# Where the time steps of a state-space layer stand: a new order at the seam of two layers in a one-core Trainium2 kernel

## The chip, the core and the metric

The kernel runs on one core of a Trainium2 chip. The metric is the device time of one execution in microseconds, as the median of several runs. Five engines work from queues of their own, each in its order: TensorE (PE in the profile, its weight loads PEld), VectorE (DVE), ScalarE (ACT), GpSimd (POOL), and SyncE (SP), which here issues most transfers. An instruction that waits holds up all that stands behind it on its engine.

## The reference

Two layers on a latent stream of 1024 tokens by 1024 features and a context of 256 tokens. Layer 0 is gated windowed attention with rotary positions. Layer 1, of which the change moves the beginning, is a gated bidirectional state-space mixer with 8 groups of 4 heads, head size 64, state size 128, chunks of 128 tokens. Cut to what matters:

```python
z, xbc, dt_raw = jnp.split(h @ w_in, [SSD_WIDTH, SSD_WIDTH + SSD_CONV_DIM], axis=-1)
xbc = jax.nn.silu(centred_depthwise_conv(xbc, conv_w, conv_b))      # 5 taps
xs, bm, cm = jnp.split(xbc, [...])
dt = jax.nn.softplus(dt_raw + dt_bias_dir)                          # time steps, 64 = 2 directions x 32 heads
...
da = dt * a_dir ; a_cs = cumsum(da) in chunks of 128                # per direction
states = einsum(bm, exp(a_last - a_cs), xs * dt)
# scans over the chunks: first the 2 of the context, then the 8 of the latents
y = y_diag + y_off ; u = (y + d_skip * xs) * silu(z) ; grouped norm ; @ w_out
```

The time steps `dt` are needed by every group; `xs`, `bm`, `cm` and `z` belong to a group.

## The kernel before

Features lie on the partitions, tokens along the free axis, in three pieces `TT`: tokens 0 to 511 (i = 0), 512 to 1023 (i = 1) and the context (i = 2). Every product is done three times in a reduced float format, high by high, high by low and low by high, so operands are split into `uH`, `uL` and `wh`, `wl`: ScalarE casts the high part, VectorE or GpSimd subtracts the low one.

The end of layer 0 is `out_steps(1)` in `attention` (L836 to L838): for each of eight output tiles it loads two weight halves (`wr`, L219, split at L212 and L214), multiplies (L226 to L228), adds the gated result to the residual `h1k` on VectorE (L760), squares it on ScalarE (L767) and adds the square to `sqa` on GpSimd (L768). Then `fin` sums the squares over partitions with a product by ones (L258), takes the root on ScalarE (L260), the reciprocal on VectorE (L261) and modulates the eight tiles of piece 1 into `uH`, `uL` (L293 to L295).

`ssd_consts` comes next. It loads the time steps' weights (`wdth`, `wdtl`), multiplies them with pieces 2, 0 and 1 into `psX` (L899, recorded as L226 to L228), evicts to `dt` (L900) and runs softplus, logarithm, scans and exponentials on the 64 rows, in tiles `w` (L906 to L952). There are two such chains, an early one over pieces 0 and 2 (768 columns) and a late one over piece 1 (512 columns). Split rows go out to DRAM (`rowh`, `rowl`, L927 to L932). At the end each chunk's values are transposed so that tokens lie on partitions: TensorE (L956, L959, L960) into `psX`, ScalarE from there into `dtdec`, `eacs` and `dtb` (L957, L961, L962). `psX` has three buffers, and a transpose into a tile waits for an earlier copy out of the same tile.

`front(g)` makes a group's inputs: tile 0 (`bT`), tiles 1 and 2 (the two halves of `xs`, through `cacc`), tile 3 (`cT`) and then z. Tiles 0 to 2 also have a context product into `psD` (24 matmuls of 256 columns, L1046); then 48 matmuls of 512 columns for the latents into `pj2` (L1055). Their finish is queued as steps in `post`: five taps (one on ScalarE L968, four on VectorE L972), silu (tanh on ScalarE L979, the product on VectorE L980), and `natural`, the transposes that put tokens on partitions (TensorE L1019, copies on ScalarE L1022). `post.run(cost)` emits steps as the front's matmuls go on, by an estimated cost of each matmul. `states(0)` follows as soon as tile 2 is done: per chunk a weighting on GpSimd (L1130), a product (L1153) and a decay and add.

The order on each engine isn't the order of this code: the program is built with `schedule_with_timeline_sim=True`, where a scheduler orders all instructions by its own estimates. `issue_after` and priorities restrict it.

Of the kernel before, what the change touches and what calls it, by code (L numbers as in the profile page):

```python
# [9 lines left out]
F32 = mybir.dt.float32  # L10
BF16 = mybir.dt.bfloat16
F32R = mybir.dt.float32r
# [5 lines left out]
P = 128  # L18
# [41 lines left out]
LATE = 3.0  # L60
SEGS = (1.5, 2.0, 2.0, 2.2, 2.2)
# [42 lines left out]
class Kernel:  # L104
# [117 lines left out]
    def mm3(self, ps, pairs, first=True, last=True):  # L222

        n = len(pairs)
        for i, (lh, ll, rh, rl) in enumerate(pairs):
            self.nc.tensor.matmul(ps, lh, rh, start=first and i == 0, stop=False)  # L226
            self.nc.tensor.matmul(ps, lh, rl, start=False, stop=False)  # L227
            self.nc.tensor.matmul(ps, ll, rh, start=False, stop=last and i == n - 1)  # L228
# [493 lines left out]
    def attention(self, c0, ckv):  # L722
# [21 lines left out]
        def out_steps(i):  # L744
# [4 lines left out]
            def one(m):  # L749
# [15 lines left out]
                else:  # L765
                    sq = t(p, [P, n], F32, "ut")
                    nc.scalar.activation(sq, h1, AF.Square)  # L767
                    nc.gpsimd.tensor_tensor(st["acc"], st["acc"], sq, op=ALU.add)  # L768
# [80 lines left out]
    def ssd_consts(self, p):  # L849
# [3 lines left out]
        dr = self.dr  # L853
# [17 lines left out]
        self.acs_d = t(dr, [2, 64, LAT], F32, "acs")  # L871
        self.v_d = t(dr, [2, 64, LAT], F32, "vrow")
# [3 lines left out]
        eal_d = t(dr, [1, 64, NT], F32, "eald")  # L876
        q = self.pdt
        wr = t(self.wp, [P, KT, P], F32, "wr")[:, :, :64]
# [15 lines left out]
        keep = keep.rearrange("p c n -> p (c n)")  # L894
        dts = t(q, [64, LAT + CTX], F32, "dt")
        where = {0: 0, 2: 512, 1: 768}
        for i in (2, 0, 1):
            n = TT[i][1]
            pj = self.proj(ps, (wh, wl), i, tag="psX", m=64)  # L899
            nc.scalar.activation(dts[:, where[i] : where[i] + n], pj[:64, :n], AF.Identity, bias=db)  # L900
        for lo, n, chunks in ((0, 768, (0, 1, 2, 3, 8, 9)), (768, 512, (4, 5, 6, 7))):
            nb = n // P
            dt = dts[:, lo : lo + n]
            if lo:
                q = self.pool("dtp2", ctx=self.cdt, side="right")
            w1, w2, w3 = [t(q, [64, n], F32, x) for x in ("w1", "w2", "w3")]  # L906

            nc.vector.scalar_tensor_tensor(w1, in0=dt, scalar=-1.0, in1=dt, op0=ALU.mult, op1=ALU.min)
            nc.scalar.activation(w1, w1, AF.Exp)
            nc.vector.tensor_scalar_add(w2, w1, 1.0)  # L910
            nc.vector.tensor_scalar_add(w3, w2, -1.0)
            nc.vector.tensor_sub(w1, w1, w3)
            nc.scalar.activation(w2, w2, AF.Ln)
            nc.scalar.activation(w3, w2, AF.Exp, scale=-1.0)
            nc.vector.tensor_mul(w1, w1, w3)
            nc.vector.tensor_add(w1, w1, w2)
            nc.vector.scalar_tensor_tensor(dt, in0=dt, scalar=0.0, in1=w1, op0=ALU.max, op1=ALU.add)
            ln = w2
            nc.vector.tensor_scalar_max(ln, dt, 1.0e-38)
            nc.scalar.activation(ln, ln, AF.Ln)  # L920
            da = w1
            nc.vector.tensor_scalar(out=da, in0=dt, scalar1=al, scalar2=None, op0=ALU.mult)
            acs = w3
            nc.vector.tensor_tensor_scan(out=acs[:32], data0=keep[:32, :n], data1=da[:32], initial=0.0, op0=ALU.mult, op1=ALU.add)
            nc.vector.tensor_tensor_scan(out=acs[32:, ::-1], data0=keep[32:, :n][:, ::-1], data1=da[32:, ::-1], initial=0.0, op0=ALU.mult, op1=ALU.add)
            def rows(dst, src):
                h = t(q, [64, 512], F32R, "rowh", 2)  # L927
                l = t(q, [64, 512], F32R, "rowl", 2)
                nc.scalar.copy(h, src[:, :512])
                nc.vector.tensor_sub(l, src[:, :512], h)  # L930
                for x, y in enumerate((h, l)):
                    nc.sync.dma_start(dst[x, :, chunks[0] * P : chunks[0] * P + 512], y.bitcast(F32))  # L932

            rows(self.acs_d, acs)
            av = acs.rearrange("p (c n) -> p c n", n=P)
            tot = t(q, [64, 6], F32, "tot")[:, :nb]
            nc.vector.tensor_copy(tot[:32], av[:32, :, P - 1])
            nc.vector.tensor_copy(tot[32:], av[32:, :, 0])
            et = t(q, [64, 6], F32, "et")[:, :nb]
            nc.scalar.activation(et, tot, AF.Exp)  # L940
            nc.sync.dma_start(eal_d[0][:, chunks[0] : chunks[0] + 4], et[:, :4])
            if nb > 4:
                nc.sync.dma_start(eal_d[0][:, 8:10], et[:, 4:])

            nc.vector.tensor_sub(ln, ln, acs)
            rows(self.v_d, ln)

            dd = w1
            nc.vector.tensor_sub(dd.rearrange("p (c n) -> p c n", n=P), tot.unsqueeze(2).broadcast_to([64, nb, P]), av)
            nc.scalar.activation(dd, dd, AF.Exp)  # L950
            nc.vector.tensor_mul(dd, dd, dt)
            nc.scalar.activation(acs, acs, AF.Exp)  # L952
# [10 lines left out]
        nc.sync.dma_start(self.eal, eal_d.broadcast_to([P, 64, NT]))  # L963
# [18 lines left out]
    def front(self, g, st, post, first=None):  # L982
# [21 lines left out]
        def need(w):  # L1004
            while "l" not in w:
                post.pop()
# [30 lines left out]
        for n, (x, kind) in enumerate(tiles):  # L1037
            need(w)
            cur, w = w, loads[n + 1]()
            nat = {"bT": ("bn", 0), 0: ("xn", 0), 1: ("xn", P)}.get(kind)  # L1040
            wh, wl = cur["h"], cur["l"]
            if nat:
                raw = t(ps, [P, 512], F32, "psD")[:, :CTX]
                for k in range(KT):
                    for y, (l, r) in enumerate(((wh, uH), (wh, uL), (wl, uH))):
                        nc.tensor.matmul(raw, l[:, k, :], r[2][:, k, :], start=k + y == 0, stop=k == KT - 1 and y == 2)  # L1046
                        yield N256
                acc = t(pf, [P, CTX], F32, "cctx")
                post.extend(self.taps(x, raw, acc, 0, CTX, CTX) + self.silu(raw, acc) + natural(raw, acc, [(st[nat[0]][2], 0, 2)], nat[1], 2))
            raw = t(ps, [P, LAT], F32, "pj2")  # L1050
            acc = t(pf, [P, LAT], F32, "cacc") if nat and kind != "bT" else t(p, [P, LAT], F32, kind)
            for k in range(KT):
                for y, (l, r) in enumerate(((wh, uH), (wh, uL), (wl, uH))):
                    for i in range(2):
                        nc.tensor.matmul(raw[:, 512 * i : 512 * i + 512], l[:, k, :], r[i][:, k, :], start=k + y == 0, stop=k == KT - 1 and y == 2)  # L1055
                        yield N512
                if k == 3:
                    post.extend(w["steps"])
# [563 lines left out]
```

## Time and profile before

| what | value |
|---|---|
| median of 3 runs (lowest to highest) | 1857.68 us (1857.05 to 1858.12) |
| the profiled execution, its own time | 1859.69 us |
| its span, first to last instruction | 1858.0 us |
| mean granted TensorE clock | 0.988 |
| TensorE busy | 1778.6 us (96%) |
| VectorE, ScalarE, GpSimd busy | 1176.4, 902.9, 731.7 us |
| layer 0's last sum of squares (L258) | at 752.7 us |
| first time-step transpose (L956) | at 793.4 us |
| tile 2 of the first front starts | at 813.9 us |
| first z product (L1080) | at 843.8 us |

How to read the rows below: a row of an engine has the start and the length in microseconds, the engine, the line of the kernel, the operation, what it writes and reads, the shape, and in brackets how long the engine was idle before it and what ended that. The row of tenths cuts the span in 40 slices, a digit being the busy tenths of a slice (9 is 90% or more); the row PEclk is the clock that TensorE was granted, in tenths. A matmul's length includes its way through the array, so matmuls in a row overlap, and what one costs is the distance between their starts. A wait is put down to what came last by the profile.

### The profile page before, as it was taken

The page shows a single profiled execution, that of the slowest core. Times are in us where ns is not written, and L with a number is a line of the kernel's source. Part 1 is how long each engine was busy: PE and PEld are TensorE (multiplying, and loading weights), DVE is VectorE, ACT ScalarE, POOL GpSimd, SP SyncE. Part 2 cuts the span into 40 slices and gives each one's busy share as a digit, 9 for nine tenths or more (in the row PEclk, how much of TensorE's full clock was granted, in tenths as well). Part 3 has the DMA queues.
Part 4 walks back from the last instruction along what each step waited for, and adds up shares of the span by engine and source line. Part 5 has one row for each costly group of instructions (what it writes and reads, how often), then busy time and mean ns, then how long its engine had stood idle before and what let it go on. Part 6 is the DMA issues. An engine that isn't in the chain of part 4 may idle for free. (4 is left out here: it accounts for less than half of the span.)

```text
span 1858.0 us, 29740 instructions
## 1 busy us (share of the span) xinstructions
PE 1778.6 (96%) x10684; PEld 1537.0 (83%) x10684; DVE 1176.4 (63%) x2208; ACT 902.9 (49%) x1858; POOL 731.7 (39%) x1007
## 2 busy tenths in 40 slices
PE   6999999999999998979999999999999999999997
PEld 4797877788898786768898898989889898988886
DVE  3654438777778666773766657576665757754743
ACT  3522336677788664552444435344443534543532
POOL 2441137654466454103252443525344352542411
PEclk9999999999999999989999999999999999999998
DMA  7767866443355447021111111111111111433552
GB/s 294 278 170 251 272 167 151 106 116 97 90 136 121 127 129 229 17 65 35 30 40 52 33 47 33 48 33 39 53 34 47 34 47 34 155 109 98 176 161 72
DMA packets 145492, 196.30 MB, mean 106 GB/s; under 512 B 15393, under 2 KB 84897, under 8 KB 144321
## 3 DMA queue, kind: packets, MB, share of 16 engines
q1 hardware_dynamic: 111280, 175.76, 30.2%
q0 software_dynamic: 34064, 18.65, 5.5%
q8 instruction: 84, 1.38, 0.3%
q14 instruction: 64, 0.52, 0.1%
HBM read 158.73 MB, written 35.92 MB: 105 GB/s over the span
## 5 line engine op out<-in xcount | busy, mean ns | idle before, releaser
L226 PE MATMUL pj<-uH,wh 128*128 128x256 f32 (+1 forms) x664 | 236.9, 357 | 5.7 <-DVE xn L1510 1.9
L228 PE MATMUL pj<-uH,wl 128*128 128x256 f32 (+1 forms) x664 | 224.5, 338 | 2.0 <-POOL wl L214 2.0
L227 PE MATMUL pj<-uL,wh 128*128 128x256 f32 (+1 forms) x664 | 224.1, 337 | 0.4 <-POOL uL L720 0.4
L1130 POOL TENSOR_TENSOR xw<-xn,dtdec 128x256 f32<-128x256 f32 x144 | 105.9, 738 | 205.4 <-PE psD L1153 102.9
L214 POOL TENSOR_TENSOR wl<-wr,wh 128x512 fp32r<-128x512 f32 x100 | 132.1, 1324 | 109.7 <-ACT wh L212 103.6
L1055 PE MATMUL pj<-uH,wh 128*128 128x512 f32 x512 | 171.7, 405 | 1.3 <-ACT xn L1022 1.3
L1055 PE MATMUL pj<-uH,wl 128*128 128x512 f32 x512 | 171.5, 404 | 0.0
L1055 PE MATMUL pj<-uL,wh 128*128 128x512 f32 x512 | 168.6, 399 | 0.0
L1080 PE MATMUL pj<-wh,uH 128*128 128x256 f32 x512 | 154.7, 302 | 0.0
L702 DVE TENSOR_TENSOR pl<-pt,ph 128x512 fp32r<-128x512 f32 x168 | 114.3, 688 | 59.7 <-ACT ph L701 58.9
L1080 PE MATMUL pj<-wh,uL 128*128 128x256 f32 x512 | 151.2, 295 | 0.0
L1080 PE MATMUL pj<-wl,uH 128*128 128x256 f32 x512 | 150.9, 295 | 0.0
L226 PEld LDWEIGHTS pj<-uH,wh 128*128 128x128 f32 x664 | 126.3, 190 | 28.8 <-issue 7.8
L212 ACT CAST wh<-wr 128x512 fp32r<-128x512 f32 (+1 forms) x140 | 89.8, 643 | 106.2 <-PE pj L227 78.1
L228 PEld LDWEIGHTS pj<-uH,wl 128*128 128x128 f32 x664 | 125.9, 190 | 17.7 <-POOL wl L214 3.2
L676 DVE CUSTOM_DVE_ANT_0 sm<-S,mask,nsink 128x640 f32<-128x640 f32 (+2 forms) x160 | 119.0, 772 | 33.7 <-PE S L673 19.7
L1259 ACT ACTIVATE uT<-psX,nw 128x128 f32<-128x128 f32 x128 | 47.0, 367 | 189.7 <-PE psX L1258 188.6
L227 PEld LDWEIGHTS pj<-uL,wh 128*128 128x128 f32 x664 | 126.6, 191 | 11.3 <-issue 1.1
L701 ACT CAST ph<-pt 128x512 fp32r<-128x512 f32 x168 | 97.6, 586 | 60.9 <-PE pt L697 54.9
L678 ACT ACTIVATE sm<-sm,nm 128x640 f32<-128x640 f32 (+2 forms) x160 | 118.5, 742 | 17.4 <-DVE nm L676 14.6
L1225 POOL TENSOR_TENSOR xs<-xn,sk 128x256 f32<-128x256 f32 x64 | 42.1, 657 | 185.1 <-DVE sk L1221 183.8
L1055 PEld LDWEIGHTS pj<-uL,wh 128*128 128x128 f32 x512 | 95.6, 188 | 19.9
(332 smaller groups left out, 5022.6 us busy)
## 6 DMA issues: line engine op xcount, KB each, us to landing
wr<-w_x SPq DMA_DIRECT2D x32, 512.0 KB
wr<-wo SPq DMA_DIRECT2D x48, 256.0 KB
wr<-w_sk SPq DMA_DIRECT2D x24, 512.0 KB
wr<-wg SPq DMA_DIRECT2D x44, 256.0 KB
qs<-q POOLq DMA_DIRECT2D x40, 256.0 KB, 3.9
wada<-w_ad SPq DMA_DIRECT2D x8, 1024.0 KB
wr<-wq SPq DMA_DIRECT2D x32, 256.0 KB
wl<-w_ada SPq DMA_DIRECT2D x32, 256.0 KB
```

The source lines that it names most:

```text
L212: nc.scalar.copy(h, raw)
L214: (eng or nc.vector).tensor_tensor(l, raw, h, op=ALU.subtract)
L226: self.nc.tensor.matmul(ps, lh, rh, start=first and i == 0, stop=False)
L227: self.nc.tensor.matmul(ps, lh, rl, start=False, stop=False)
L228: self.nc.tensor.matmul(ps, ll, rh, start=False, stop=last and i == n - 1)
L676: nc.vector.tensor_tensor_reduce(out=sm[:, :W], in0=Sv, in1=self.mask[:, m0 : m0 + W], scale=-SCALE, scalar=self.nsink[:, 4 * j + r : 4 * ...
L678: nc.scalar.activation(sm[:, :W], sm[:, :W], AF.Exp, bias=nm[:, r : r + 1], scale=-1.0, accum_out=sums[:, r : r + 1])
L701: nc.scalar.copy(ph, ptf)
L702: nc.vector.tensor_sub(pl, ptf, ph)
L1055: nc.tensor.matmul(raw[:, 512 * i : 512 * i + 512], l[:, k, :], r[i][:, k, :], start=k + y == 0, stop=k == KT - 1 and y == 2)
L1080: nc.tensor.matmul(pj[:, c], l, r[:, k, :], start=c % 2 + q + k + y == 0, stop=c % 2 == 1 and q == 1 and k == 3 and y == 2)
L1130: nc.gpsimd.tensor_tensor(xw, X(st, c).rearrange("p (r h) -> p r h", r=R), self.dtdec[:, c, hd(d, g)].unsqueeze(2).broadcast_to([P, R, HP] ...
```

## The change

Five edits.

1. The time steps' setup (weights, bias, `al`, `keep`) moves from `ssd_consts` to `dt_setup`, which is called ahead of `out_steps(1)`, in layer 0's attention scope. The context's time-step product `dt_proj(2, "pt")` is issued after the last output tile's matmuls and ahead of the sum of squares. The last square is added on VectorE instead of GpSimd.
2. The two chains become `dt_chain`, which returns a function for the transposes. `ssd_consts` returns `spread`, which calls both and loads `eal`. It is called once 30 us of estimated front cost (`DTLATE`) have gone by.
3. The rows `rowh`, `rowl` have one buffer instead of two.
4. The first front (g = 0) does context 0, tile 0 for piece 0, tile 1 for piece 0, tile 0 for piece 1, context 1, tile 1 for piece 1. Other fronts keep their order.
5. `sz` gets a pool of its own, opened with `scan` after the spread; the row constants and the first row load move there too.

```diff
-                    nc.gpsimd.tensor_tensor(st["acc"], st["acc"], sq, op=ALU.add)
+                    (nc.vector if i == 1 and m == KT - 1 else nc.gpsimd).tensor_tensor(st["acc"], st["acc"], sq, op=ALU.add)
...
-            for f in out_steps(1):
+            steps = out_steps(1)
+            self.dt_setup()
+            for f in steps[:-1]:
                 for _ in f():
                     pass
+            with self.tc.issue_after(self.mm.ins):
+                mm = self.dt_proj(2, "pt")
+            with self.tc.issue_after(mm.ins):
+                for _ in steps[-1]():
+                    pass
...
+        self.dt_proj(0, "psX")
+        self.dt_proj(1, "psX")
+        early = self.dt_chain(0, 768, (0, 1, 2, 3, 8, 9))
+        late = self.dt_chain(768, 512, (4, 5, 6, 7))
+
+        def spread():
+            early()
+            late()
+            nc.sync.dma_start(self.eal, self.eal_d.broadcast_to([P, 64, NT]))
...
+    def dt_proj(self, i, tag):
+        n, o = TT[i][1], {0: 0, 2: 512, 1: 768}[i]
+        pj = self.proj(self.psA, self.wdt, i, tag=tag, m=64)
+        mm = self.mm
+        self.nc.scalar.activation(self.dts[:, o : o + n], pj[:64, :n], AF.Identity, bias=self.db)
+        return mm
...
-                h = t(q, [64, 512], F32R, "rowh", 2)
-                l = t(q, [64, 512], F32R, "rowl", 2)
+            h = t(q, [64, 512], F32R, "rowh", 1)
+            l = t(q, [64, 512], F32R, "rowl", 1)
...
+        if g == 0:
...
+            yield from context(0, w0)
+            r0 = tokens(tiles[0][1])
+            yield from mm(r0[0], w0, both[:1])
...
+            r1 = tokens(tiles[1][1])
+            yield from mm(r1[0], w1, both[:1])
+            yield from mm(r0[0], w0, both[1:])
+            finish(0, *r0)
+            yield from context(1, w1)
+            yield from mm(r1[0], w1, both[1:])
+            finish(1, *r1)
+            n = 2
...
-            sz = t(p, [P, 4, 256], F32, "sz")
+            sz = t(self.pz, [P, 4, 256], F32, "sz")
...
-        for cost in self.front(0, st, post):
+        work = self.front(0, st, post)
+        while done < DTLATE:
+            cost = next(work)
+            post.run(cost)
+            done += cost
+        spread()
+        self.cdt.close()
+        self.pz = self.pool("sz", ctx=c0)
+        ps2 = self.pool("scan", ctx=c0)
```

Since a scheduler sets the order, here is what came of it. First TensorE from tile 1's last matmul (`pj_2228` before, `pj_2212` after) to tile 2's first (`pj_2235`), before the change; the `psX` rows are time-step transposes, `psD_9114` is tile 1's context product, `cacc` is tile 1, `rrow` the first decays:

```order
L1055 MATMUL pj_2228_9147<-uH_2144_8675,wl_9087 128x512
L956 MATMUL psX_8882<-ident_63,w_2177_8840 128x64
...
L959 MATMUL psX_8882<-ident_63,w_2179_8842 128x64
...
L956 MATMUL psX_8981<-ident_63,w_2192_8919 128x64
L1046 MATMUL psD_9114<-uH_1735_7025,wh_9085 128x256
...
L1019 MATMUL pj_2228_9147<-ident_63,cacc_9148 128x128 x4
L1189 MATMUL psX_9702<-rrow_8998 128x256 x2
...
L1019 MATMUL pj_2228_9147<-ident_63,cacc_9148 128x128 x4
L1055 MATMUL pj_2235_9256<-uH_2057_8255,wh_9194 128x512
```

The same place after it (`pj_2209` and `bT` are tile 0; `w_2177` and `w_2179` belong to the early chain, `w_2186` and `w_2188` to the late one; `cctx_9093` is tile 1's context):

```order
L1074 MATMUL pj_2212_9011<-uH_2155_8721,wl_8955 128x512
L988 MATMUL psX_9171<-ident_63,w_2177_8840 128x64
...
L991 MATMUL psX_9171<-ident_63,w_2179_8842 128x64
...
L991 MATMUL psX_9192<-ident_63,w_2179_8842 128x64
...
L1052 MATMUL pj_2209_8973<-ident_63,bT_8974 128x128 x4
L988 MATMUL psX_9205<-ident_63,w_2186_8885 128x64
...
L1052 MATMUL pj_2209_8973<-ident_63,bT_8974 128x128 x4
L991 MATMUL psX_9205<-ident_63,w_2188_8887 128x64
...
L1052 MATMUL psD_9061<-ident_63,cctx_9093 128x128 x2
L1074 MATMUL pj_2235_9259<-uH_2057_8255,wh_9124 128x512
```

The transposes still stand together ahead of tile 2. Between them now stand tile 0's natural transposes, which need `bT` finished; tile 1's context product and the first decays are gone from here, the one to a place ahead, the other to one behind.

Second ScalarE, from the last square of layer 0 (`ut`) to the first modulated tile of piece 1 (`uH_2144` before, `uH_2155` after); before:

```order
L767 ACTIVATE ut_8667<-h1k_8638 128x512
L260 ACT_TABLE_LOAD
L260 ACTIVATE sqa_8672<-pj_8670,eps_70 128x512
L294 ACTIVATE uH_2144_8675<-h1k_8331,mod_6_75 128x512
L900 ACTIVATE dt_8761<-psX_8762,db_8751 64x256
```

and after:

```order
L768 ACTIVATE ut_8687<-h1k_8658 128x512
L924 ACTIVATE dt_8338<-pt_8690,db_8328 64x256
L261 ACT_TABLE_LOAD
L261 ACTIVATE sqa_8718<-pj_8716,eps_70 128x512
L295 ACTIVATE uH_2155_8721<-h1k_8351,mod_6_75 128x512
```

The eviction of the context's time steps has moved from behind the first modulated tile to a place ahead of the root's table load.

Later stages of the program show only small exchanges of neighbouring instructions.

More of the change, by code (lines that the diff above doesn't have):

```diff
@@ L1036, in front @@
             post.extend(w["steps"])
[L1037 to L1049, printed above, removed]
-            raw = t(ps, [P, LAT], F32, "pj2")
[L1051 to L1058, printed above, removed]
```

194 lines of the change are left out of this document (120 added, 74 removed).

## The prediction

> **What bounds the kernel now.** I read the page first, then busy time by stage, then TensorE's waits in the stretch that the change touches, then each engine's own row of instructions there. The page:
>
> ```profile
> PE   6999999999999998979999999999999999999997
> PEclk9999999999999999989999999999999999999998
> ```
>
> Outside its two ends TensorE has one weak place: the 8 and the 7 of its row, the 16th and 18th slice (697 to 743 and 790 to 836 us, at 46.45 us a slice), where the layers meet; right there the granted clock dips too. What is saved on TensorE there reaches the end, because TensorE is full afterwards. The stages of that place (columns: length, then busy time and instructions of PE, PEld, DVE, ACT, POOL, then clock, DMA share, GB/s):
>
> ```profile
> 753.30:792.50 39.20, 39.20 (x196) 30.41 (x194) 35.08 (x50) 27.13 (x35) 0.00 (x0) 1.00 0.04 9
> 792.50:805.10 12.60, 4.49 (x28) 3.45 (x27) 11.02 (x14) 9.60 (x35) 0.00 (x0) 0.61 0.52 133
> 805.10:813.86 8.76, 6.41 (x38) 5.97 (x37) 8.72 (x13) 6.80 (x12) 0.00 (x0) 0.78 0.02 6
> ```
>
> In the second and third row TensorE is half idle and VectorE (DVE) is full: 11.02 of 12.60, 8.72 of 8.76. Its costliest wait between 740 and 1000 us (total, times, longest):
>
> ```profile
> PE psX L959 <- ACT dtdec L957: 7.2, 2, 6.9
> ```
>
> It names ScalarE's copy of a transposed time step; that copy stands late in ScalarE's queue, behind a chain that runs back and forth between ScalarE and VectorE. So the hole at 793 to 814 us is set by how much VectorE has to do before it, and the question is whether the new order puts less there.
>
> **Part 1, the last output tile.** TensorE's wait before the sum of squares (L258) is filled with the context's time-step product, 24 matmuls of 256 columns.
>
> ```profile
> 752.71 1.12 PE L258 MATMUL pj<-sqa,ones 128*128 128x512 f32 x2 [2.99 <-POOL sqa L768]
> 754.02 0.27 PE L226 MATMUL psX<-uH,wdth 128*64 128x256 f32 x1
> 754.14 0.28 PE L227 MATMUL psX<-uL,wdth 128*64 128x256 f32 x1
> ...
> 751.27 1.28 ACT L260 ACT_TABLE_LOAD   x1
> 753.87 0.69 ACT L260 ACTIVATE sqa<-pj,eps 128x512 f32<-128x512 f32 x1 [1.32 <-PE pj L258]
> 759.40 0.46 ACT L900 ACTIVATE dt<-psX,db 64x256 f32<-64x256 f32 x1
> ...
> 754.59 3.35 DVE L261 RECIPROCAL sqa<-sqa 128x512 f32<-128x512 f32 x1 [4.09 <-ACT sqa L260]
> ```
>
> These matmuls start 0.12 us apart (the second and third row): 24 of them are some 2.8 us, from 749.6 to 752.4, so they fit the gap of 2.99 almost exactly, and the last add, now on VectorE and shorter there, is over by then. TensorE gains 2.8 us here. But the product's eviction (L900, 0.46 us on ScalarE) now stands ahead of the square root's table load. It can't start before 752.5, so the load runs 753.0 to 754.3 instead of 751.27 to 752.55, under the wait. Square root at 754.3 instead of 753.87: the reciprocal, and with it all of VectorE's work behind it, starts 0.4 us later, at 755.0. The 2.8 us aren't kept either: ahead of the time-step transposes TensorE now also does the second tile's context product (24 matmuls of 256 columns, 2.8 us), which stood behind them. It reaches the transposes at about 792, as before. Sum of this part: 0 for TensorE, 0.4 us late for VectorE. The Trainium skill (ScalarE: Activation LUTs, What ACT_TABLE_LOAD costs) counts 1.28 us for the load and another 1.38 of drain; by that the root would come at 755.7. No drain shows in the rows of this trace (third rival), so the sum uses 1.28.
>
> **Part 2, the hole.** TensorE's row has the transposes, then tile 0's transposes to natural layout (L1052, of bT), then tile 2. In order, TensorE can't start tile 2 before bT's last product on VectorE. What VectorE does before, from rows of the old trace:
>
> ```profile
> 774.48 0.42 DVE L980 SCALAR_TENSOR_TENSOR cctx<-psD,cctx 128x256 f32<-128x256 f32 x1 [1.36 <-ACT psD L979]
> 775.08 0.68 DVE L908 SCALAR_TENSOR_TENSOR w<-dt 64x512 f32<-64x512 f32 x1 [0.18 <-ACT dt L900]
> ...
> 781.81 0.68 DVE L915 TENSOR_TENSOR w<-w,w 64x512 f32<-64x512 f32 x1 [1.04 <-ACT w L914]
> ...
> 789.90 1.21 DVE L999 TENSOR_TENSOR wl<-wr,wh 128x1024 fp32r<-128x1024 f32 x1
> ...
> 798.40 0.68 DVE L930 TENSOR_TENSOR rowl<-w,rowh 64x512 fp32r<-64x512 f32 x1 [0.41 <-ACT rowh L929]
> 799.01 0.68 DVE L951 TENSOR_TENSOR w<-w,dt 64x512 f32<-64x512 f32 x1
> ...
> 806.40 1.27 DVE L972 SCALAR_TENSOR_TENSOR bT<-pj,cw,bT 128x1022 f32<-128x1022 f32 x1
> 807.64 1.23 DVE L980 SCALAR_TENSOR_TENSOR cacc<-pj,cacc 128x1024 f32<-128x1024 f32 x1
> ...
> 833.55 1.51 DVE L972 SCALAR_TENSOR_TENSOR cctx<-psD,cw,cctx 128x255 f32<-128x255 f32 x3
> ```
>
> From the reciprocal (754.59) to the end of the late chain's last product (799.69) are 45.1 us, with 1.36 + 0.18 + 1.04 + 0.41 = 3.0 idle: 42.1 of work. In the new order all of it but that last product (0.6 from start to start) precedes bT's product, and besides it a low weight part (1.2), four taps and the product of bT and two taps of tile 1 (7 x 1.2, from 806.40 to 807.64), and four taps of the second context (4 x 0.4): 11.2. For idle time I take 1.3 us, between none and the old 3.0: by its new order ScalarE has seven table loads in this stretch instead of nine, and convolution work fills waits. One new wait may add to it: the time steps' rows (rowh, rowl) have one buffer instead of two, so the second split waits until the first has been written out.
>
> ```profile
> 805.11 1.41 SPq L1178 DMA_DIRECT2D rraw<-vrow  x2
> ...
> 808.15 0.83 ACT L1181 CAST rrow<-rraw 32x768 fp32r<-32x768 f32 x1 [0.55 <-DMA rraw<-vrow]
> ```
>
> A small transfer lands 1.6 us after its issue (806.5 to 808.1). Between the two high splits ScalarE has a table load and two small activations (2.1 us), between the two low ones VectorE has four operations (3.5 us) and SP two more issues: covered but for some 0.5 us, which is in the 1.3. Without that cover each split would hold up its engine by 2 us, and on VectorE the low weights and bT behind it. 755.0 + 42.1 - 0.6 + 11.2 + 1.3 = 809.0 (807.7 to 810.7).
>
> From there the old trace shows the same steps, though ScalarE was late for two of them:
>
> ```profile
> 811.90 0.66 PE L1019 MATMUL pj<-ident,cacc 128*128 128x128 f32 x4 [1.05 <-ACT xn L1022]
> 813.86 0.72 PE L1055 MATMUL pj<-uH,wh 128*128 128x512 f32 x2 [1.30 <-ACT xn L1022]
> ...
> 811.27 0.57 ACT L1022 COPY xn<-pj 128x512 f32<-128x512 f32 x1
> ```
>
> Two transposes (2 x 0.66) and two copies (2 x 0.57) with hand-overs are 2.6 us: tile 2 starts at 811.6 instead of 813.86, 2.2 us earlier. It starts on a slow clock, after some 9 us with little to do. The old trace shows what that costs:
>
> ```profile
> 800.66 0.36 PE L959 MATMUL psX<-ident,w 64*128 64x64 f32 x1 [6.90 <-ACT dtdec L957]
> 805.90 0.41 PE L1046 MATMUL psD<-uH,wh 128*128 128x256 f32 x1
> 806.11 0.41 PE L1046 MATMUL psD<-uL,wh 128*128 128x256 f32 x1
> ...
> 809.07 0.28 PE L1046 MATMUL psD<-uH,wh 128*128 128x256 f32 x1
> ...
> 810.14 0.71 PE L1189 MATMUL psX<-rrow 128*128 128x256 f32 x4
> ...
> 842.20 0.66 PE L1019 MATMUL pj<-ident,cacc 128*128 128x128 f32 x4 [1.61 <-ACT xn L1022]
> ```
>
> After the wait of 6.90 us these start 0.21 apart until 809, instead of the 0.12 of the context's product: 17 matmuls at 0.09 more, 1.6 us. There the loss lay under VectorE's work; now it falls on tile 2. And the first decay products (L1189, 4 matmuls in 0.7 us), which stood in the hole, come behind tile 2: 0.7 more. From tile 2 on nothing else is new: the wait ahead of the z part (1.61) returns in the same pattern, since its second transposes again wait for a copy, and the three state products that now precede z leave from behind it. Hole: -2.2 + 1.6 + 0.7 = +0.1, so nothing.
>
> **Part 3, the output projection before it.** No matmul changes, but the squares' adds move behind the weights on GpSimd.
>
> ```profile
> 734.63 3.00 POOL L768 TENSOR_TENSOR sqa<-sqa,ut 128x512 f32<-128x512 f32 x2 [1.95 <-ACT sqa L764]
> 737.59 1.27 POOL L214 TENSOR_TENSOR wl<-wr,wh 128x512 fp32r<-128x512 f32 x1
> ...
> 738.91 0.50 PE L228 MATMUL pj<-uH,wl 128*128 128x512 f32 x1 [1.33 <-POOL wl L214]
> ...
> 736.17 0.62 ACT L212 CAST wh<-wr 128x512 fp32r<-128x512 f32 x1 [1.00 <-DMA wr<-wo]
> ```
>
> The seventh tile's low weights waited behind two adds although their high part was ready at 736.8. Without the adds they start 0.8 us sooner, and TensorE's wait of 1.33 shrinks by that: -0.8. The adds, now later, must be through when VectorE adds the last one at 751.3; seven operations of 1.3 us after 740 end by about 749.6, so they are. Bounds: the whole wait goes (-1.3), or the two w_x loads that now stand ahead of a weight half on SP's queue cost what the second rival says (+3.5). The small loads and the setup of the time steps move into this stage: one 256 KB load leaves the crowded part, which is worth at most its share; I put it at 0. The z pool changes addresses only: 0, covered by the nines of TensorE's row.
>
> **Sum.** 0 + 0.1 - 0.8 = -0.7 us against the profiled execution (span 1858.0, its own time 1859.69, which is 2.0 over the median of 1857.68). Taken from the median: 1857.0. A difference of 0.2% is 3.7 us, about what can be told from no change here. For the forecast I allow the hole -3 to +2.5 (the bounds of the idle time and of the clock) and the projection -1.3 to +1.
>
> **Rivals.** Two of them need rows of their own, the crowded stage (DMA share and GB/s stand last) and a table load on ScalarE:
>
> ```profile
> 720.00:740.00 20.00, 16.07 (x64) 10.96 (x63) 13.49 (x15) 11.48 (x18) 10.90 (x8) 1.00 0.79 286
> ```
>
> ```profile
> 796.36 1.28 ACT L940 ACT_TABLE_LOAD   x1
> 797.65 0.20 ACT L940 ACTIVATE et<-tot 64x4 f32<-64x4 f32 x1
> ```
>
> - *VectorE keeps ahead* (chance 0.27, faster). If VectorE's short operations fill ScalarE's gaps so well that bT's product ends by 804, tile 2 starts near 806.6 (804 + 2.6), 5.0 us sooner than forecast: 1852.0. For it: VectorE idled 3.0 us in this chain, and ScalarE loads two tables less. Against: 755.0 and the 52.7 us of work alone (42.1 - 0.6 + 11.2) make 807.7; 804 needs shorter operations as well.
> - *The weights come late* (0.12, slower). In the crowded stage of the output projection, two 512 KB loads of w_x are issued one weight half earlier than before, so two halves of w_o each have 0.5 MB more ahead of them. At the stage's 286 GB/s that is 1.8 us each. If TensorE can't make it up at the seventh tile, 3.5 us with nothing saved: 1861.2. It decides from the point at which a half arrives over 1.3 us late, since that is the wait it can use up. For it: the seventh tile's cast, quoted above, did wait 1.00 for w_o. Against: TensorE waited 1.33 there anyway, so a late fifth tile uses that up first.
> - *A table load costs twice its length* (0.04, within 0.2%). If ScalarE stood idle after each load for as long as the load takes (1.28 us), the root would come 1.3 us later and all of VectorE's work with it: 1858.3. Against it stands the old trace, with 0.02 us between a load's end and the next activation where that one is ready (loaded 796.36 to 797.64, activation at 797.65). It is what the Trainium skill's figure (ScalarE: Activation LUTs, same section) would make of it.
> - *The change doesn't do what it says* is in part my forecast: the transposes still stand in a row ahead of tile 2, with a convolution's result now in between, so the hole is moved and not filled. Chance of the forecast: 0.57.
>
> **The numbers.** Faster by over 0.2% 0.28: the first rival and a little of the forecast's lower end. Slower 0.15: the second rival, and the case that the hole and the projection both lie at their upper bounds. The rest, 0.57, is within. The range 1851.0 to 1860.3 reaches from just past the first rival to just short of the second.
>
> **What would show it.** In the new profile the wait at L258 is under 0.3 us, and the context's product stands ahead of it. TensorE reaches the transposes between 790.5 and 792.5 (span's clock), waits longest for VectorE's product of bT (L1013) at the natural transposes, for 7 to 10 us, and starts tile 2 at 809 to 813 with 512-column matmuls more than 0.35 us apart at first. The z part starts at 842 to 845 with four state products done. If tile 2 starts before 808, or the longest wait is under 5 us, my VectorE sum is wrong; if the context's product in the gap costs more than 3 us, the first part is.

## The result and the profile after

The changed kernel takes 1879.53 us (median of 4, 1876.04 to 1881.09) beside 1857.9 us for the kernel before on the same chip: a ratio of 1.0106, 95% interval 1.0089 to 1.0122, so some 20 us slower. The forecast of 1857.0 and its range to 1860.3 are wrong, and none of the rivals was it. The profiled execution took 1881.09 us, with a span of 1879.4.

The page of the changed kernel, TensorE's tenths and its clock:

```profile
PE   6999999999999999879999999999999999999997
PEclk9999999999999999979999999999999999999998
```

Outside the two ends there is still one weak place: the 8 and the 7 now stand together in the 17th and 18th slice, where the layers meet, and the rest looks as full as before. In tenths of a slice of 47 us nothing shows that would cost 20 us. So I went on to finer stretches. The changed kernel's busy time (columns as in the prediction's rows of stages):

```profile
1100.00:1200.00 100.00, 97.06 (x617) 87.92 (x616) 65.74 (x118) 42.40 (x87) 37.35 (x58) 0.98 0.13 38
1200.00:1300.00 100.00, 97.51 (x587) 86.32 (x587) 66.53 (x115) 43.04 (x87) 33.94 (x50) 0.98 0.13 37
1640.00:1670.00 30.00, 26.03 (x120) 19.64 (x119) 20.61 (x42) 13.14 (x27) 20.48 (x29) 0.94 0.26 70
```

and the kernel before in the same stretches:

```profile
1100.00:1200.00 100.00, 99.51 (x646) 90.54 (x645) 69.18 (x126) 47.61 (x97) 41.73 (x63) 1.00 0.13 39
1200.00:1300.00 100.00, 99.51 (x624) 89.65 (x623) 66.42 (x124) 42.86 (x87) 38.41 (x58) 1.00 0.13 38
1640.00:1670.00 30.00, 30.00 (x147) 25.02 (x146) 13.30 (x26) 9.46 (x17) 10.10 (x15) 1.00 0.28 78
```

TensorE starts 29 and 37 matmuls less per 100 us in the middle of the groups, and 27 less in 30 us where the last group meets the output projection, and its clock dips there. No edit touches these places. Over the whole span, 21.4 us longer, TensorE is idle for 9.9 us more and busy for 11.5 us more (1790.1 against 1778.6) with the same 10684 matmuls, so the waits alone aren't the whole loss. Its waits behind the first front, from 850 us to the end (total, times, longest; those that only the changed kernel has):

```profile
PE pj L1150 <- ACT xn L1055: 3.0, 2, 2.1
PE pj L1074 <- ACT bn L1055: 2.3, 3, 0.8
PE psX L1245 <- DVE y L1294: 2.1, 3, 1.5
...
PE pj L1052 <- ACT xn L1055: 0.9, 1, 0.9
PE pj L1052 <- ACT bn L1055: 0.8, 1, 0.8
```

L1055 is ScalarE's copy of natural tiles out of `pj2` (L1022 before). TensorE waits for it 7.3 us in eight places, seven of them of 0.7 us or more; in the kernel before it does so nowhere behind the first front.

Times of the first z product of a group, counted from layer 0's last sum of squares (L258, L259 after), show where the loss builds up (us; the last column is from the eighth z product to the span's end):

| kernel | tile 2 | first z | eighth z | eighth z to the end |
|---|---|---|---|---|
| before | 61.2 | 91.1 | 842.9 | 262.4 |
| after | 62.9 | 96.2 | 855.8 | 272.4 |

1.7 us at tile 2 and 5.1 at the first z (three more state products stand ahead of it); then 7.8 more over the seven groups, and 10.0 behind the last front. Not all of the 5.1 is lost: experiment 1 has the same seam and is 4.5 late at the first z, but 1.8 at the eighth.

### The profile page after: what moved, and what is told of

Its sections match the earlier page's. It is cut to its first block, busy times and chain, and to the rows that moved or that the text cites. A ratio compares the mean times of both kernels' runs of the same rounds, so it can differ in the third digit from the quotient of the medians.

```text
span 1879.4 us, 29772 instructions
## 1 busy us (share of the span) xinstructions
PE 1790.1 (95%) x10684; PEld 1539.8 (82%) x10684; DVE 1184.4 (63%) x2209; ACT 898.5 (48%) x1856; POOL 728.3 (39%) x1006
## 3 DMA queue, kind: packets, MB, share of 16 engines
q8 instruction: 84, 1.38, 0.3%
## 5 line engine op out<-in xcount | busy, mean ns | idle before, releaser
L1186 POOL TENSOR_TENSOR xw<-xn,dtdec 128x256 f32<-128x256 f32 x144 | 94.8, 661 | 294.6 <-PE psD L1209 110.9
L227 PEld LDWEIGHTS pj<-uH,wh 128*128 128x128 f32 x664 | 127.0, 191 | 29.6 <-issue 9.8
L229 PEld LDWEIGHTS pj<-uH,wl 128*128 128x128 f32 x664 | 126.6, 191 | 15.8 <-issue 1.1
L228 PEld LDWEIGHTS pj<-uL,wh 128*128 128x128 f32 x664 | 127.3, 192 | 11.3 <-issue 1.1
L1074 PEld LDWEIGHTS pj<-uH,wh 128*128 128x128 f32 x512 | 95.0, 189 | 22.9 <-ACT bn L1055 3.8
L1074 PEld LDWEIGHTS pj<-uH,wl 128*128 128x128 f32 x512 | 95.7, 189 | 19.3 <-DVE wl L1032 0.5
```

The source lines that it names most:

```text
L229: self.mm = self.nc.tensor.matmul(ps, ll, rh, start=False, stop=last and i == n - 1)
L1074: nc.tensor.matmul(raw[:, o : o + n], l[:, k, :], r[i][:, k, :], start=k + y == 0, stop=k == KT - 1 and y == 2)
L1186: nc.gpsimd.tensor_tensor(xw, X(st, c).rearrange("p (r h) -> p r h", r=R), self.dtdec[:, c, hd(d, g)].unsqueeze(2).broadcast_to([P, R, HP] ...
```

## The experiments

The question is which of the edits' effects loses the 20 us. Theory A: the scheduler laid out everything behind the first front anew, and that order costs. B: the seam itself loses, and the rest is late by it. C: the z pool's addresses.

In the built programs the kernel before repeats itself: from the second group's scan to the sixth's TensorE's row is the same, without one difference. In the changed kernel two neighbouring groups differ in 41 to 68 places. The traces show the same: from one group's first z to the next TensorE does 682 matmuls in 108.6 us in each group from the second on before the change, and 650 to 690 in 103.7 to 115.6 us after it. To separate order from edit, a helper takes the order of each engine from the other kernel's built program and ties an instruction to the one ahead of it (an order of issue only, no wait):

```diff
+def pin(tc, mark):
...
+        row = [q[k + d] for k, d in enumerate(moved)]
+        for x, y in zip(row, row[1:]):
+            tc.add_manual_dep(y, x.name, mybir.DependencyInfo(mybir.DependencyClass.NoSync, mybir.DependencyReason.DATA), reason="issue_after")
...
+        pin(self.tc, self.mark)
```

`mark` is the point in the code behind the first front, `moved` the table of places for an engine. Ratios below are to the kernel before, run beside each, with 95% intervals.

**1. The new seam with the old order behind it.**

> The changed kernel with all its edits, but from the first front's end on every engine gets its instructions in the order of the kernel before (edges that set the order only, no waits of their own). Theory A, the loss is in the order that the scheduler gave the later groups and the output projection: 1857 to 1862 us, the seam's own difference alone (the first z product was 3.5 us late). Theory B, the seam itself loses it and everything behind is late by it: about 1879, as the changed kernel. Theory C, the z pool's new addresses cost something in each group: about 1879.

Measured: 0.9999 (0.9989 to 1.0009). All five edits are in, and the time is that of the kernel before, within some 2 us. A holds, B and C fall.

**2. The old seam with the new order behind it.** The same helper in the kernel before, with the table of the changed kernel.

> The kernel before with none of the edits, but from the first front's end on every engine gets its instructions in the order of the changed kernel. Theory A: 1872 to 1879 us. Theory B: 1858. Theory C: 1858.

Measured: 1.0116 (1.0098 to 1.0134). The order alone makes the whole loss.

**3. The two small edits.**

```diff
-            sz = t(p, [P, 4, 256], F32, "sz")
+            sz = t(self.pz, [P, 4, 256], F32, "sz")
...
+        self.pz = self.pool("sz", ctx=c0)
...
-                h = t(q, [64, 512], F32R, "rowh", 2)
-                l = t(q, [64, 512], F32R, "rowl", 2)
+                h = t(q, [64, 512], F32R, "rowh", 1)
+                l = t(q, [64, 512], F32R, "rowl", 1)
```

> The kernel before with two of the small edits only: the pool of its own for sz and one buffer instead of two for rowh and rowl. No product, transpose or setup moves in the code. The scheduler gives the later groups the changed kernel's order with these two already. Theory A: 1872 to 1880 us. Theory B: 1858, since none of the seam's edits is in. Theory C: about 1876, since the pool is in.

Measured: 1.0097 (1.0082 to 1.0113). Two edits that move no operation in the code give the loss, by the scheduler's answer to them: in the traces the order from the first z product on is the changed kernel's, instruction by instruction, on TensorE, VectorE, ScalarE and GpSimd.

**4. The z pool alone.** The first of the two pairs of lines above, and the line that opens the pool.

> The kernel before with the pool of its own for sz alone; the scheduler's order behind the seam is that of the kernel before. Theory A: 1857 to 1859 us. Theory B: 1858. Theory C: about 1876.

Measured: 0.9996 (0.9984 to 1.0008). The pool by itself is free, as the prediction had it; C falls for good.

**5. The rows alone.** The second pair.

> The kernel before with one buffer instead of two for rowh and rowl, and nothing else; the order of TensorE behind the seam stays that of the kernel before. If the time goes by the order and not by the edit: 1857 to 1860 us. If the single buffer costs by itself: up to 4 us more (each of two splits waits 2 us for the write of the one before).

Measured: 1.0019 (1.0007 to 1.0032), 3.5 us. The order behind the seam stays that of before, and the buffer costs by itself (1 to 6 us by the interval). Experiments 11 and 12 take this up.

**6. TensorE's order alone.** As experiment 1, with only TensorE tied.

> The changed kernel with all its edits; from the first front's end on TensorE alone gets its instructions in the order of the kernel before, the other engines are left to the scheduler. If it is TensorE's order that costs the time: 1857 to 1862 us, as with all five engines. If the other engines' order carries part of it: 1865 us or more.

Measured: 0.9994 (0.9983 to 1.0004). With TensorE's old order the other engines fall in by themselves; in the trace they too have the old order.

**7. The copies that TensorE waits for.** The changed kernel's own order on every engine; seven of ScalarE's copies stand further ahead, six by one place and one by three.

```diff
+UP = {19: 1, 25: 3, 28: 1, 33: 1, 36: 1, 46: 1, 52: 1}
...
+                row.insert(k - UP.get(n, 0), row.pop(k))
```

> The changed kernel with all its edits and its own order on every engine, except that behind the first front seven of ScalarE's 63 copies of natural tiles (those for which TensorE waited 0.7 to 2.1 us) stand one to three places further ahead in ScalarE's queue. In the changed kernel's profile these waits are 6.95 us in all, and some stretches of slow clock follow them. If it is these copies that cost the time in the groups: 1869 to 1873 us, since the eighth z product comes 7 to 9 us sooner. If each wait only makes room for the next: 1877 to 1880.

Measured: 1.0058 (1.0045 to 1.0071) against 1.0106 with the copies where they were: 8.9 us come back from seven moves in one queue. The worst of the seven, in the changed kernel (ScalarE, then TensorE):

```profile
1158.71 1.04 ACT L1028 CAST wh<-wr 128x1024 fp32r<-128x1024 f32 x1
1159.65 0.56 ACT L1001 ACTIVATE cctx<-psD,cb,cw 128x256 f32<-128x256 f32 x1
1160.11 0.81 ACT L1237 CAST rrow<-rraw 32x768 fp32r<-32x768 f32 x1
1160.83 0.50 ACT L1302 ACTIVATE y<-y,ss 128x256 f32<-128x256 f32 x1
1161.24 0.56 ACT L1055 COPY xn<-pj 128x512 f32<-128x512 f32 x1
...
1159.02 0.60 PE L1052 MATMUL pj<-ident,cacc 128*128 128x128 f32 x4
1161.85 0.39 PE L1150 MATMUL pj<-wh,uH 128*128 128x256 f32 x1 [2.12 <-ACT xn L1055]
```

The transposes are through at 1159.62, but the copy stands behind a context tile's first tap, the row constants and a scan's scaling, all ready at the time. The z product needs the copied tile's buffer and waits 2.12 us. The same place in the kernel before:

```profile
1158.72 1.21 ACT L968 ACTIVATE cT<-pj,cb,cw 128x1024 f32<-128x1024 f32 x1 [0.19 <-PE pj L1055]
1159.83 0.57 ACT L1022 COPY xn<-pj 128x512 f32<-128x512 f32 x1
```

There the copy is next in the queue, and TensorE had other work between the transposes and z. The Trainium skill (PSUM — Partial Sum Buffer, Engine vs sequencer instructions) calls ScalarE's queue a strict FIFO; the trace agrees, the ready copy passes nothing. With the copies moved up, the waits for L1055 (L1084 there) fall from 7.3 to 2.3 us:

```profile
PE pj L1179 <- ACT xn L1084: 0.9, 2, 0.6
...
PE pj L1081 <- ACT xn L1084: 0.5, 1, 0.5
...
PE pj L1103 <- ACT bn L1084: 0.3, 1, 0.3
PE pj L1081 <- ACT bn L1084: 0.3, 1, 0.3
PE pj L1103 <- ACT xn L1084: 0.3, 1, 0.3
```

The eighth z comes 848.8 us behind the sum of squares instead of 855.8; from there to the end it is 271.5, as in the changed kernel (272.4). That is 7.0 of the 11.1 us that the new order loses up to there (the eighth z is at 844.7 in experiment 1, with the same seam). The saving is more than the 5.0 us of shorter waits: the clock, which is at half for 3.41 us three times between 850 and 1750 us in the changed kernel, stays whole there. The copies are the larger part of the loss in the groups; what costs the other 4 us there no run shows, and the loss behind the eighth z has a second cause.

**8. Where the other half comes from: the last group's own order.**

> The kernel before with none of the edits; only from the last group's scan on (the eighth group and the output projection beside it) every engine gets its instructions in the order of the changed kernel, all earlier groups keep theirs. In the run with the whole new order behind the seam 9 of the 18 us were lost up to the eighth z product and 9 behind it. If the two losses are independent: 1865 to 1869 us. If the last stage only loses because the groups hand it a late state: 1858 to 1860.

> The changed kernel with all its edits and its own order, except that from the last group's scan on every engine has the order of the kernel before. The last group's new order alone lost nothing in the kernel before. If the 10 us behind the eighth z product come from what the earlier groups hand over (state products put off past the front): 1876 to 1881 us, as the changed kernel. If they need the last group's own new order as well: 1867 to 1871.

Measured: 0.9990 (0.9978 to 1.0003) and 1.0107 (1.0093 to 1.0121). The last group's new order is free if the groups ahead keep the old one, and its old order saves nothing behind new groups. The loss is handed over by the groups ahead. In the changed kernel TensorE has no product with streamed weights for 16.1 us (1646.8 to 1662.9), only these and their like:

```profile
1646.79 0.40 PE L1547 MATMUL pj<-uH,wl 128*128 128x512 f32 x1
...
1649.27 0.50 PE L1245 MATMUL psX<-rrow 128*128 128x256 f32 x2 [1.54 <-DVE y L1294]
1649.69 0.67 PE L1209 MATMUL psD<-xw,bn 128*128 128x256 f32 x2
1651.38 1.06 PE L1209 MATMUL psD<-xw,bn 128*128 128x256 f32 x2
...
1654.04 0.67 PE L1209 MATMUL psD<-xw,bn 128*128 128x256 f32 x2
1655.82 0.70 PE L1209 MATMUL psD<-xw,bn 128*128 128x256 f32 x2
...
1662.93 0.50 PE L1547 MATMUL pj<-uH,wh 128*128 128x512 f32 x1
```

These are state products of the eighth group (L1209), about 2 us apart, with GpSimd's weighting of the next and its decay of the state between them, and with two scan slots. Behind the last matmul of the eighth z part seven state products are left here, from 1643 to 1661 us; in the kernel before three, from 1634 to 1645, with products of the output projection between them.

**9. The eighth front with the old order.** From the seventh group's scan on, which emits the eighth front and its states.

> The changed kernel with all its edits and its own order up to the scan of the seventh group (counted from one); from there on, the eighth front and its state products with it, every engine has the order of the kernel before. If the 10 us behind the eighth z product are the state products that the new order puts off past the last front: 1867 to 1871 us. If they come from elsewhere: 1876 to 1881.

Measured: 1.0075 (1.0061 to 1.0090), 6 us less than with the new order to the end. In its profile the part behind the eighth z is 262.7 us, that of the kernel before (262.4), and the stretch of 16 us is gone; the eighth z is at 856.0, as in the changed kernel. By its median of 1873.4 us the run lies between the two forecasts. So the second cause lies in the order of this part, and the time gained is less than the 10 us of the profile. That it is the late state products themselves is how the rows read; no run moves them alone.

**10. Both repairs together.**

> Both repairs together, and the rest of the new order kept: the copies on ScalarE that TensorE waited for further ahead in its queue, and the order of before from the seventh group's scan on. If these two causes are the loss: 1858 to 1863 us, level with the kernel before. If a third is left: 1865 or more.

Measured: 1.0064 (1.0049 to 1.0080). It is the second case, and the two repairs don't give the time back. Behind the eighth z all is well (264.2 us), but from the seventh z to the eighth it takes 119.2 us instead of 108.6: at the joint of the two orders TensorE again has no front product for a while (6.0 us at 1528.8, 3.6 at 1535.8), with late states and scan slots in its row, and the clock is at half for 10.2 us from 1533.2 on. The joint is of the experiment's own making, so how the remaining 10 us divide is not settled. Experiments 8 to 10 fit late states that cost wherever the front work ends first, but don't prove it.

**11. The seam itself: what its edits are worth.** With the old order behind the first front, first without the filled wait (the context's product back behind the sum of squares, the last square on GpSimd), then with two buffers for `rowh` and `rowl`.

> The changed kernel with the order of before from the first front's end on, and with the context's time-step product back behind the sum of squares (the last square added on GpSimd again); the spread and the first front's order stay. If the filled wait is worth nothing, since VectorE sets the seam, as predicted: the same as with it, 1857 to 1861 us. If its 2.8 us are kept: 2 to 3 us slower than with it.

> The changed kernel with the order of before from the first front's end on, and with two buffers for rowh and rowl as before (cT is allocated in the z pool, to make room). The prediction put the single buffer at some 0.5 us in the new seam: 1857 to 1861 us, as with one buffer. If it costs what it cost alone in the kernel before: 3 us faster, 1854 to 1857.

Measured: 0.9996 (0.9988 to 1.0005) and 0.9988 (0.9979 to 0.9998), against 0.9999 with the fill and one buffer. The filled wait is worth nothing that can be told (about 2 us could be), as predicted. Two buffers gain some 2 us; the intervals overlap, but it agrees with the single buffer's cost alone (experiment 5), and in the profile the eighth z comes at 840.8 us behind the sum of squares instead of 844.7. The move of `cT` is in that too.

**12. A better seam.** VectorE sets the hole, so the late chain is called later, and held behind bT's product on VectorE and behind tile 2's first matmuls on TensorE.

```diff
+            with self.tc.issue_after(self.bt.ins), self.tc.issue_after(self.fmm.ins):
+                self.dt_chain(768, 512, (4, 5, 6, 7))()
...
+        for part, until in ((early, 27.0), (spread, 34.0)):
```

> The changed kernel with the order of before from the first front's end on, and with the late chain of time steps (piece 1) moved on VectorE behind bT's product and its transposes behind tile 2's matmuls; early transposes directly behind tile 1. If VectorE's work ahead of bT sets the hole, as predicted, some 14 operations of 0.6 us leave it: tile 2 starts at 803 to 807 instead of 812 us, and the time is 1851 to 1856. If ScalarE's part of the chains, the weights or the buffers set it: tile 2 at 810 or later, 1857 to 1862.

> The fastest kernel so far (late chain behind bT's product, order of before from the first front's end on) with two buffers for rowh and rowl, cT in the z pool. If ScalarE's and VectorE's splits waited for the rows' writes ahead of bT: 1848 to 1851 us. If those waits are covered: 1851 to 1854.

Measured: 0.9952 (0.9939 to 0.9965) with one row buffer, 0.9941 (0.9928 to 0.9953) with two; the second, 1848.99 us, is the fastest version. With one buffer tile 2 starts at 804.3 and the time is 1851.84 us, both as forecast for VectorE's work setting the hole. Its last early time-step transposes, natural transposes and tile 2 at the seam (TensorE):

```profile
795.05 0.57 PE L1008 MATMUL psX<-ident,w 64*128 64x64 f32 x2 [4.36 <-ACT dtb L1014]
795.80 1.12 PE L1072 MATMUL pj<-ident,bT 128*128 128x128 f32 x4 [0.18 <-DVE bT L1033]
...
799.38 1.22 PE L1094 MATMUL pj<-uH,wh 128*128 128x512 f32 x2 [0.25 <-ACT bn L1075]
```

TensorE waits 0.18 us for bT's product where the changed kernel waits 10.7 (its longest wait there is now 4.36, for ScalarE's copies of the early time steps), and tile 2 starts 49.6 us behind the sum of squares instead of 62.9 (55.8 with one buffer). Without the tied order it doesn't show:

> The kernel with the late chain behind bT's product, as in the fastest run so far, but with the scheduler's own order behind the first front, which is one of those that don't repeat from group to group. If such orders cost what the changed kernel's does: 1867 to 1875 us, the seam's gain of 7 us eaten by a loss of 15 to 20. If only the changed kernel's own order is bad: 1850 to 1856.

Measured: 1.0062 (1.0043 to 1.0082): the scheduler gives this seam another order that doesn't repeat, and a loss of 20 us is back.

## Why the prediction was wrong, point by point

**The step that failed** is in Part 2: "From tile 2 on nothing else is new". It took the later groups to be as before, because they were full before ("TensorE is full afterwards"), and so the sum was carried to the end unchanged. The section on the change had the hint, "small exchanges of neighbouring instructions", and read it too lightly: with 650 to 690 matmuls to a group instead of 682, work has moved from one group into the next. Such an order decides what stands ahead of a copy that TensorE waits for, and how many state products are left for the end. Priced by the runs, the order behind the first front is +21.6 us (1.0116). "The z pool changes addresses only: 0" is right for the pool (0.9996) and wrong for the change, since together with the single row buffer it tips the scheduler's order (1.0097).

**What bounds the seam** was read rightly: VectorE's work ahead of bT's product. TensorE's rows of the changed kernel there, with the longest wait where it was forecast:

```profile
750.94 0.28 PE L228 MATMUL pt<-uL,wdth 128*64 128x256 f32 x1
751.05 0.28 PE L229 MATMUL pt<-uH,wdtl 128*64 128x256 f32 x1
751.17 1.02 PE L259 MATMUL pj<-sqa,ones 128*128 128x512 f32 x2
...
792.58 0.40 PE L988 MATMUL psX<-ident,w 64*128 64x64 f32 x3 [1.52 <-DVE w L980]
...
810.01 1.11 PE L1052 MATMUL pj<-ident,bT 128*128 128x128 f32 x4 [10.72 <-DVE bT L1013]
...
814.02 1.20 PE L1074 MATMUL pj<-uH,wh 128*128 128x512 f32 x2
```

**Part 1** was right. The wait at the sum of squares is gone, the context's product stands in it, and TensorE reaches the transposes at 791.1 (790.5 to 792.5 was said) and starts them at 792.6, behind a wait of 1.52 us for VectorE. The root has no drain ahead of it:

```profile
751.37 0.47 ACT L924 ACTIVATE dt<-pt,db 64x256 f32<-64x256 f32 x1 [1.31 <-PE pt L229]
751.86 1.28 ACT L261 ACT_TABLE_LOAD   x1
753.15 0.69 ACT L261 ACTIVATE sqa<-pj,eps 128x512 f32<-128x512 f32 x1
```

The table load ends at 753.14 and the root starts at 753.15, so the third rival falls. The 1.38 us of drain in the Trainium skill (ScalarE: Activation LUTs, What ACT_TABLE_LOAD costs) are not to be seen here either.

**Part 2, the hole.** Wait 10.7 us (7 to 10 was said), tile 2 at 814.0 (809 to 813), first z at 847.4 (842 to 845), each past its range, with four state products ahead of z, as said. In the same seam of experiment 1 tile 2 is at 812.3 and z at 845.2, but there layer 0 ends 1.6 us sooner. The sum from reciprocal to bT's product was 54.0 us and measured 56.1. The term that was too small is VectorE's idle time: put at 1.3 us, 0.5 of it for the single row buffer, it is 3.9. The row buffer takes 2.06 of it and one wait for an exponential on ScalarE, behind its table load, 1.86; the work is 0.5 us less than said. VectorE's rows:

```profile
753.88 3.35 DVE L262 RECIPROCAL sqa<-sqa 128x512 f32<-128x512 f32 x1 [3.02 <-ACT sqa L261]
...
774.05 0.95 DVE L944 TENSOR_TENSOR w<-w,w 64x768 f32<-64x768 f32 x1 [1.86 <-ACT w L943]
...
789.18 0.68 DVE L959 TENSOR_TENSOR rowl<-w,rowh 64x512 fp32r<-64x512 f32 x1 [0.50 <-DMA acs<-rowl]
...
808.14 0.68 DVE L959 TENSOR_TENSOR rowl<-w,rowh 64x512 fp32r<-64x512 f32 x1 [1.56 <-DMA acs<-rowl]
808.75 1.21 DVE L1013 SCALAR_TENSOR_TENSOR bT<-pj,bT 128x1024 f32<-128x1024 f32 x1
```

In both chains the second split waits for the write of the first, 2.06 us in all, and the later wait stands directly ahead of bT's product. The four operations of VectorE that were counted as cover did lie ahead of it, but the write took longer than the 1.6 us that were read off a small transfer. With two buffers (experiment 11) these waits are gone and the sum is 51.3 us. SyncE's rows:

```profile
803.84 0.33 SPq L889 DMA_DIRECT2D eal<-eald  x1
804.26 0.45 SPq L961 DMA_DIRECT2D acs<-rowl  x1
```

It was issued 0.4 us behind the 320 KB load of `eal` and had landed at 808.1, 3.9 us later; the early chain's write, issued at 786.83, had landed at 789.2. Whether the load held up the later one, no run shows. From bT's product to tile 2 it is 4.1 us instead of 2.6: at half clock four of tile 0's transposes take 1.1 us instead of 0.66, and time-step transposes stand between them. The term for tile 2's own slow clock was right: until 817.9 its matmuls are 0.43 us apart.

**Part 3** had the sign right; its size can't be read from one pair of profiles. The sum of squares is at 751.2 instead of 752.7, but the six profiles with the old end of layer 0 have it at 749.2 to 755.1 (mean 751.9), the eleven with the filled wait at 747.8 to 753.6 (mean 750.1). The gain is nearer 2 us than 0.8. The w_x loads of the second rival did no harm: TensorE's waits for weights in the projection were no longer than before, the longest 1.14 us.

**The sum** of the edits alone was -0.7 us, and experiment 1, which has them all and the old order behind, measures -0.2 (-2.0 to +1.7). It agrees in part by luck: in the profiles the stretch from the sum of squares to the end is 2.2 us longer than before (1107.5 against 1105.3; the hole was put at +0.1), and the stretch ahead of it some 2 us shorter. And it is of no use for the time of the changed kernel, in which the scheduler's answer weighs thirty times as much.

**The rival that was missing** was the order itself: the section on the kernel says that a scheduler orders everything by its own estimates, so a change of the order far behind the edit should have stood there with a price. The rows to price it from are in the old trace: TensorE's waits from 850 us on come to 13.2 us, 7.1 of them at the program's end and none for a copy, so a new order had little to win there and more to lose.

## What to carry to other kernels

Where a scheduler sets the order, an edit's price has two parts: what it moves, and what the scheduler makes of everything behind it. Compare the built order far from the edit, ask whether a loop that repeated still repeats, and look at what now stands ahead of each result that the bounding engine waits for. Tying the rest of the program to its old order tells the two parts apart in one run, and a gain at one place (here 0.6%) may only show once that is done.

## What the runs showed of the hardware

A wait of 2.12 us was enough to bring TensorE's clock down. In these traces the granted clock changes only on a grid of steps of 3.41 us. The steps with the wait at 1161.85 and with three shorter ones (0.94, 0.32 and 0.18 us) ahead of 1275.31, each with the step behind it, in the changed kernel:

```profile
1159.26:1162.67 3.41, 1.29 (x11) 1.05 (x10) 3.41 (x6) 3.33 (x8) 0.17 (x1) 1.00 0.01 2
1162.67:1166.08 3.41, 3.41 (x19) 3.41 (x18) 3.34 (x5) 1.42 (x2) 0.00 (x0) 0.50 0.59 179
...
1271.90:1275.31 3.41, 1.97 (x13) 1.31 (x12) 3.41 (x6) 3.41 (x10) 0.40 (x1) 1.00 0.18 70
1275.31:1278.72 3.41, 3.41 (x11) 2.88 (x12) 3.41 (x8) 2.06 (x4) 0.86 (x1) 0.50 0.49 137
```

For the whole step behind such waits the clock is at half and 256-column matmuls are 0.21 us apart instead of 0.12, so a wait costs more than its length. The Trainium skill (TensorE: Matmul & The Clock Gate, The HAM clock gate) puts the fall after an idle window of about 3.4 us. Here TensorE was busy for 1.29 and 1.97 us of the step before the fall. The 2.99 us ahead of the old sum of squares (749.72 to 752.71) brought no fall; they lie across two steps:

```profile
747.57:750.98 3.41, 2.15 (x10) 1.43 (x8) 0.75 (x1) 0.36 (x1) 0.06 (x1) 1.00 0.00 0
750.98:754.39 3.41, 1.68 (x9) 1.15 (x10) 0.00 (x0) 2.07 (x3) 1.26 (x1) 1.00 0.20 77
```

So the length of a wait alone doesn't decide it, nor does the busy time of a step: 1.97 us were followed by a fall, 1.68 were not. Small transposes stand in the two steps that were, and none in these; what counts isn't settled by the runs.
